# Keeping x in SBUF through layer 0 and passing gate rows through DRAM in a two-block fp32 transformer kernel

## The chip, the cores and the metric

One core of one Trainium2 chip runs the whole program. The metric is the device time of one launch in microseconds (us); less is better. The trace names the engines PE (TensorE, matmuls), PEld (its weight loads), DVE (VectorE), ACT (ScalarE), POOL (GpSimd) and SP (SyncE). A DMA is issued by an instruction in one of the queues; the rows ACTq and SPq are such issues.

## The reference

All is fp32, with 256 latent tokens (x), 256 context tokens (cx) and a model width D of 1024. A first block of two layers attends over both; a second block of two layers has ffn, mix, ffn. Cut to what matters here:

```python
def layer(x, cx, ...):                        # first block, twice
    mod = c_silu @ ada_w + ada_b              # shift, scale, gate: 1024 each
    shift, scale, gate = jnp.split(mod, 3, axis=-1)
    hx = rmsnorm(x, norm_w) * (1 + scale[:, None, :]) + shift[:, None, :]
    ...                                       # three kinds of attention -> ux, uc
    x = x + gate[:, None, :] * (ux @ w_out)
    if need_ctx:                              # layer 0 alone
        cx = cx + gate_c * (uc @ w_out)

def second_block(x, ...):                     # twice
    x = x + 0.5 * swiglu(rms(x, ffn1_norm), wg, wu, wd)
    h = rms(x, mix_norm)
    (q_a, g_a, kc, vc, ...) = split_cols(h @ w_in)
    y_a = nsa(...)    # compresses kc and vc: gelu(flat @ w1) @ w2
    y_b = moba(...)
    x = x + (sigmoid(gate_a) * y_a + sigmoid(gate_b) * y_b) @ w_out
    x = x + 0.5 * swiglu(rms(x, ffn2_norm), ...)
return rms(x, final_norm)
```

## The kernel before

The weights of all products come as one stream of tiles, mostly 128x1024 words (512 KB), in the order of a plan. `_dma` (L260) puts the fetch of a tile `ws` into SP's queue, at most four tiles ahead of the splits. `_split` splits a tile into a rounded part `wh`, cast by ACT (L286), and a rest `wl = ws - wh`, by DVE (L287), two tiles ahead of their use; there are three buffers of each, so a cast waits until PE is done with the tile three before it. For each weight block `three` issues three matmuls: wh with the high part of the activations (L426), wl with the high part (L427), wh with the low part (L428). PE works through the stages in order: the two layers of the first block (in the trace to about 752 us), then ffn1, mix and ffn2 of both layers of the second block. A scheduler at build time orders the instructions of each engine from their dependencies and from which pool's memory is free. So a row of an engine's stream need not stand where its line is called.

Three places bear on the change:

- **The end of a layer of the first block** (`w_out`). Matmuls over the gated attention output fill four accumulators; `add` multiplies each by the gate row (DVE, `tmp`, L1123) and adds it to x or cx (L1124). The gate is held as a column per 128 values, `mod`. To get it as a row on every partition, L1116 multiplies each column, spread over 128 columns, with the identity, and DVE copies the result to the tile `gt` (L1117). In layer 0 the gated products of the attention (names `sg`) live in the memory of x, of cx and of one more tile; `uc` (L1107 on ACT, L1108 on DVE) are the parts of them for the context tokens, and x and cx are loaded again from DRAM (L1110) before `add`.
- **The start of mix.** Its first product `h @ w_in` needs x transposed: PE turns 128x128 blocks of x with the identity (L467), ACT and DVE split them into `xt` (L474, L475). The weights of the compression, two tiles `w1` of 128x2048 words and a small `w2`, are fetched from ACT's queue in the text's order at the start of mix (L1205, L1218); the `w1` tiles share tags (`big0`, `big1`) with later tiles of mix.
- **The pools.** `sink` and `nsink` are two tiles of 8 words a partition; the row `fw2` of the final norm is fetched at the second stage of the second block (L1518).

Of the kernel before, what the change touches and what calls it, by code (L numbers as in the profile page):

```python
# [19 lines left out]
P = 128  # L20
# [4 lines left out]
HD = 64  # L25
# [203 lines left out]
class Body:  # L229
# [526 lines left out]
    def ada_close(self, g):  # L756

        nc = self.nc
        nb = len(g["blocks"])
        self.uid += 1  # L760
        m = self.junk.tile([P, 512], F32, tag="junk", name=f"mod{self.uid}")
        nc.scalar.copy(m[:4 * nb, :], g["bank"][:4 * nb, :])
        p = self.ps("r")
        for j in range(4):
            nc.tensor.matmul(p[:, 16 * j:16 * j + 2 * nb], m[:4 * nb, j * P:(j + 1) * P],
                             self.cst("sel2")[:4 * nb, :2 * nb], start=True, stop=True)
        pv = p[:, :64].rearrange("p (j b s) -> p s b j", b=8, s=2)
        b = 0
        while b < nb:
            l, c0 = g["blocks"][b]  # L770
            e = b + 1
            while e < nb and g["blocks"][e] == (l, c0 + 512 * (e - b)):
                e += 1
            for s in range(2):
                o = c0 // P
                nc.vector.tensor_tensor(self.mod[l][:, s, o:o + 4 * (e - b)].rearrange("p (b j) -> p b j", j=4),
                                        pv[:, s, b:e, :],
                                        self.col("ada_b", 24 * l + o, 4 * (e - b)).rearrange("p (b j) -> p b j", j=4), op=ALU.add)
                a, z = max(o, 8), min(o + 4 * (e - b), 16)
                if a < z:  # L780
                    nc.vector.scalar_tensor_tensor(self.mod[l][:, s, a:z], self.mod[l][:, s, a:z], 1.0,
                                                   self.col("norm_w", 8 * l + a - 8, z - a), op0=ALU.add, op1=ALU.mult)
            b = e

    def norm_rows(self, x, dst):
# [34 lines left out]
    def block1(self, x):  # L820
        nc, tc = self.nc, self.tc
        cx = self.cx1
        with ExitStack() as es:
            hp = es.enter_context(tc.tile_pool(reuse_waits="tile", name="hT", bufs=1))
            hT = self.new_hT(hp, 0)
            with tc.tile_pool(reuse_waits="tile", name="w0", bufs=START_TILES) as self.w0:
                self.start(x, cx, hT)
            for l in range(DEPTH):
                if l:
                    self.psum("L1")  # L830
                hT = self.layer1(l, x, cx, hT, hp)

    def start(self, x, cx, hT):

# [7 lines left out]
        nc.vector.tensor_copy(self.ident_r, self.ident)  # L842
        self.norm_rows(x, x)
        self.norm_rows(cx, cx)

        def half(h):
            for c in (4 * h, 4 * h + 2):
                for s, v in enumerate((x, cx)):
                    self.mod_pair(0, s, c, self.turn_pair(v, c), hT)
# [31 lines left out]
    def layer1(self, l, x, cx, hT, hp):  # L881
# [3 lines left out]
        with ExitStack() as lay:  # L885
            lp = lay.enter_context(tc.tile_pool(reuse_waits="tile", name=f"lay{l}", bufs=1))
            if need:
                sg2 = lp.tile([P, 4, T], F32, name="sg2")
                xv, cv = (t.rearrange("p t (a d) -> p (t a) d", d=T) for t in (x, self.cx1))

                def sg(c, n):
                    return (xv, cv, sg2)[c // 4][:, c % 4:c % 4 + n, :]
            else:
                sg2 = lp.tile([P, 4, T], F32, name="sg2b")
                cv1 = self.cx1.rearrange("p t (a d) -> p (t a) d", d=T)

                def sg(c, n, sg2=sg2, cv1=cv1):
                    return cv1[:, c:c + n, :] if c < 8 else sg2[:, c - 8:c - 8 + n, :]
# [10 lines left out]
            qn = lp.tile([P, 2, HD], F32, name=f"qn{l}")  # L909
            sink = lp.tile([P, 8], F32, name=f"sink{l}")  # L910
            nc.scalar.dma_start(qn[:, 0, :], self.row_bcast(self.dram["k_norm_a"], l * HD, HD))
            nc.scalar.dma_start(qn[:, 1, :], self.row_bcast(self.dram["q_norm_a"], l * HD, HD))
            nc.scalar.dma_start(sink, self.row_bcast(self.dram["sink_c"], l * 8, 8))
            nsink = lp.tile([P, 8], F32, name=f"nsink{l}")
            nc.vector.tensor_scalar(nsink, sink, -1.0, None, op0=ALU.mult)
# [184 lines left out]
            with tc.tile_pool(reuse_waits="tile", name=f"wo{l}", bufs=1) as wp:  # L1100
                gate = wp.tile([P, 2, D], F32, name=f"gt{l}")
                tmp = wp.tile([P, 4, 512], F32, name=f"tmp{l}")
                if need:
                    uc = [wp.tile([P, 12, 256], F32R, name=f"uc{j}") for j in range(2)]
                    for c in [c for ks in WOUT_KS for c in ks]:
                        g = sg(c, 1)[:, 0, 256:512]
                        nc.scalar.copy(uc[0][:, c, :], g)  # L1107
                        nc.vector.tensor_tensor(uc[1][:, c, :], g, uc[0][:, c, :].bitcast(F32), op=ALU.subtract)  # L1108
                    for t, nm in ((x, "x"), (cx, "ctx")):
                        nc.sync.dma_start(t, self.dram[nm].rearrange("o (t p) d -> p (o t) d", p=P))  # L1110
                for s in range(2 if need else 1):
                    for ct in range(2):
                        p = self.ps("x")
                        for j in range(4):
                            g = self.mod[l][:, s, 16 + 4 * ct + j:17 + 4 * ct + j]
                            nc.tensor.matmul(p[:, j * P:(j + 1) * P], g.to_broadcast([P, P]), self.ident, start=True, stop=True)  # L1116
                        nc.vector.tensor_copy(gate[:, s, ct * 512:ct * 512 + 512], p)  # L1117

# [25 lines left out]


    def ffn(self, l, name, x, xt, ss, hooks, after):

        nc, tc = self.nc, self.tc
        with tc.tile_pool(reuse_waits="tile", name=f"f{name}{l}", bufs=1) as fp, tc.tile_pool(reuse_waits="tile", name=f"g{name}{l}", bufs=2) as gp, \
# [5 lines left out]
            for fi, (c0, n) in enumerate(FFN_COLS):  # L1155
                a = self.gemm(name + "_wg_2", l, c0, xt[0], xt[1], toks, KD, hooks if fi == 0 else None)
                if r is None:
                    r = ss() if callable(ss) else self.finish_rstd(ss, 2)
                s = gp.tile([P, 2, 512], F32, tag="s", name=f"s{name}{l}{fi}")
                for t in range(2):  # L1160
# [27 lines left out]
    def mix(self, l, x, xt, ss, hooks, after):  # L1188
        nc, tc = self.nc, self.tc
        with ExitStack() as es:  # L1190
# [11 lines left out]
            toks = [(0, None), (1, None)]  # L1202
            w1 = [op.tile([P, 16, P], F32, tag=f"big{j}", name=f"w1{l}_{j}") for j in range(2)]
            for j, nm in enumerate(("cmpk_w1_2", "cmpv_w1_2")):
                nc.scalar.dma_start(w1[j], self.dram[nm][l].rearrange("(m p) j -> p m j", p=P))  # L1205
            oT = {k: [op.tile([P, 4, 256], F32R, name=f"o{k}{l}_{j}") for j in range(2)] for k in "NM"}
# [8 lines left out]
            Vb = mp.tile([64, 2, 4, 64], F32, name=f"Vb{l}")  # L1215
            w2 = mp.tile([P, 2, HD], F32, name=f"w2{l}")
            o2 = COLS["w2"][0] + P * l
            nc.scalar.dma_start(w2, self.dram["cols"][:, o2:o2 + P].rearrange("p (a d) -> p a d", a=2))  # L1218
            graw = []
# [201 lines left out]
            for mi, (kind, b) in enumerate(MIX):  # L1421
# [7 lines left out]
                if kind in ("ga", "gb"):  # L1429
                    while len(graw) < 2:  # L1430
                        graw.append(op.tile([P, 2, D], F32, tag=f"big{len(graw)}", name=f"graw{l}_{len(graw)}"))
                    for t in range(2):
# [60 lines left out]
    def block2(self, x, out):  # L1493
# [18 lines left out]
        for i, (l, s) in enumerate(stages):  # L1512
            ss = first_scale if i == 0 else ops[i][1]
            args = (x, ops[i][0], ss, {4: lambda i=i: self.b2_half(i, 1)} if i else None, lambda h, i=i: self.b2_half(i + 1, h))
            self.psum(s)
            if i == 1:
                fw = bp.tile([P, D], F32, tag="xtrow", name="fw2")
# [17 lines left out]
    def run(self, out):  # L1535
        nc, tc = self.nc, self.tc
        with ExitStack() as es:
# [14 lines left out]
            self.ident = self.cst("ident")  # L1552
            self.ident_r = cp.tile([P, P], F32R, name="ident_r")
            self.mod = [cp.tile([P, 2, 24], F32, name=f"mod{l}") for l in range(DEPTH)]

# [74 lines left out]
```

## Time and profile before

| | before |
|---|---|
| time, median of 3 runs | 1947.4 us (1946.05 to 1948.95) |
| the profiled execution's own time | 1947.63 us |
| its span in the trace | 1945.8 us |
| PE busy | 1904.4 us, 98% of the span |
| DVE, ACT busy | 1279.4 us (66%), 1103.3 us (57%) |
| DMA | 294.62 MB, mean 151 GB/s |

The span runs from the first to the last recorded instruction; 1.8 us of the execution's time lie around it. PE's busy time is that of modelled ends, so 98% says that PE is nearly always fed, and not that it runs at its peak.

### The profile page before, as it was taken

To read this page: it belongs to the slowest core of one execution; us is meant where nothing else is said; L and a number is where in the kernel's file an instruction comes from. 1 tells how busy PE (TensorE), PEld (TensorE's weight loads), DVE (VectorE), ACT (ScalarE), POOL (GpSimd) and SP (SyncE) were. 2 spreads that over 40 slices of the span, in tenths; PEclk is the share of its full clock that TensorE was granted. 3 is DMA by queue.
4 is the path that set the end of the run, shared out by engine and by line. 5 is a ranking of instruction groups with operands and counts; after the bars stand their busy time and mean duration, and the time that the engine had idled before them with its cause. 6 is when DMAs were issued, how large, how long until landed. Compare 5 with 4: busy or idle time off the path is not lost.

```text
span 1945.8 us, 27694 instructions
## 1 busy us (share of the span) xinstructions
PE 1904.4 (98%) x10348; PEld 1561.0 (80%) x10348; DVE 1279.4 (66%) x2490; ACT 1103.3 (57%) x1979; POOL 1.0 (0%) x7
## 2 busy tenths in 40 slices
PE   8999999999999999999899999999999899999998
PEld 3777778777988877888788878888888788888886
DVE  5486856788596787555689575555555588675555
ACT  4367657775567675444467645445444458655443
POOL 0000000000000000000000000000000000000000
PEclk9999999999999999999999999999999999999999
DMA  7333324135422236554523565554555433456552
GB/s 304 106 123 130 118 90 150 55 131 186 136 93 95 85 109 216 184 184 141 166 93 125 164 215 198 183 191 173 193 186 173 144 106 101 152 180 234 186 181 74
DMA packets 85270, 294.62 MB, mean 151 GB/s; under 512 B 10000, under 2 KB 10384, under 8 KB 85136
## 3 DMA queue, kind: packets, MB, share of 16 engines
q1 hardware_dynamic: 80432, 283.39, 43.0%
q10 hardware_dynamic: 4704, 9.47, 1.5%
q8 instruction: 81, 1.33, 0.3%
q14 instruction: 53, 0.43, 0.1%
HBM read 291.77 MB, written 1.05 MB: 150 GB/s over the span
## 4 chain that ended last, share of the span: by engine, by line
PE 92%; DVE 4%; ACT 2%; issue 1%; ACTq 1%; DMA 1%; SPq 0%; DVEq 0%
PE acc L426 24%; PE acc L428 24%; PE acc L427 24%; PE pso L609 4%; PE pst L580 4%; PE pss L514 2%; PE pss L515 2%; PE psr L715 1%; DVE wl L287 1%; PE psx L1173 1%; ACT wh L286 1%; PE psr L721 1%; PE psm L747 1%; PE psm L1260 1%; PE acc L750 1%
## 5 line engine op out<-in xcount | busy, mean ns | idle before, releaser
L287 DVE TENSOR_TENSOR wl<-ws,wh 128x1024 fp32r<-128x1024 f32 (+2 forms) x538 | 638.1, 1188 | 478.8 <-ACT wh L286 476.0
L286 ACT CAST wh<-ws 128x1024 fp32r<-128x1024 f32 (+2 forms) x538 | 549.2, 1024 | 573.3 <-PE acc L428 503.3
L426 PE MATMUL acc<-wh,xt 128*128 128x512 f32 (+3 forms) x1120 | 419.6, 376 | 11.7 <-ACT wh L286 11.7
L427 PE MATMUL acc<-wl,xt 128*128 128x512 f32 (+3 forms) x1120 | 416.6, 372 | 0.0
L428 PE MATMUL acc<-wh,xt 128*128 128x512 f32 (+3 forms) x1120 | 416.4, 373 | 0.0
L426 PEld LDWEIGHTS acc<-wh,xt 128*128 128x128 f32 x1120 | 212.1, 190 | 44.9 <-ACT wh L286 12.9
L428 PEld LDWEIGHTS acc<-wh,xt 128*128 128x128 f32 x1120 | 211.8, 189 | 33.0 <-issue 0.7
L427 PEld LDWEIGHTS acc<-wl,xt 128*128 128x128 f32 x1120 | 212.7, 190 | 31.2 <-issue 0.3
L426 PE MATMUL acc<-wh,hT 128*128 128x384 f32 (+2 forms) x480 | 159.6, 333 | 0.1
L427 PE MATMUL acc<-wl,hT 128*128 128x384 f32 (+2 forms) x480 | 158.5, 330 | 0.0
L428 PE MATMUL acc<-wh,hT 128*128 128x384 f32 (+2 forms) x480 | 158.1, 329 | 0.0
L550 ACT ACTIVATE p<-pss,nm 128x512 f32<-128x512 f32 (+2 forms) x240 | 127.5, 539 | 20.3 <-DVE nm L546 5.1
L426 PE MATMUL acc<-wh,hffn 128*128 128x512 f32 x352 | 137.7, 391 | 0.0
L428 PE MATMUL acc<-wh,hffn 128*128 128x512 f32 x352 | 137.1, 389 | 0.0
L427 PE MATMUL acc<-wl,hffn 128*128 128x512 f32 x352 | 137.0, 389 | 0.0
L580 PE MATMUL pst<-consts,p 128*128 128x128 f32 x624 | 103.3, 278 | 0.0
L427 PEld LDWEIGHTS acc<-wl,hT 128*128 128x128 f32 x480 | 90.6, 189 | 7.2 <-issue 1.9
L426 PEld LDWEIGHTS acc<-wh,hT 128*128 128x128 f32 x480 | 90.5, 189 | 6.8 <-issue 0.8
L428 PEld LDWEIGHTS acc<-wh,hT 128*128 128x128 f32 x480 | 90.5, 189 | 5.8 <-issue 1.2
L580 PEld LDWEIGHTS pst<-consts,p 128*128 128x128 f32 x624 | 72.2, 140 | 28.5 <-ACT p L572 5.6
L572 ACT ACTIVATE p<-p,rinv 128x256 f32<-128x256 f32 (+2 forms) x152 | 81.5, 573 | 16.5 <-DVE rinv L566 12.2
L428 PEld LDWEIGHTS acc<-wh,hffn 128*128 128x128 f32 x352 | 66.1, 188 | 13.9
(318 smaller groups left out, 2868.5 us busy)
## 6 DMA issues: line engine op xcount, KB each, us to landing
ws<-in_wall SPq DMA_DIRECT2D x476, 512.0 KB, 3.4
ws<-in_wall SPq DMA_DIRECT2D x64, 384.0 KB, 3.1
bias<-in_bias ACTq DMA_DIRECT2D x8, 512.0 KB, 4.0
x<-in_x SPq DMA_DIRECT2D x2, 1024.0 KB, 6.5
cx<-in_ctx SPq DMA_DIRECT2D x2, 1024.0 KB, 10.3
ws<-in_wall SPq DMA_DIRECT2D x4, 420.0 KB, 3.0
out<-y SPq DMA_DIRECT2D x2, 512.0 KB, 2.6
ws<-in_wall SPq DMA_DIRECT2D x2, 280.0 KB, 2.8
```

The source lines that it names most:

```text
L286: self.nc.scalar.copy(h[:, :n], s[:, :n])
L287: self.nc.vector.tensor_tensor(lo[:, :n], s[:, :n], h[:, :n].bitcast(F32), op=ALU.subtract)
L426: mm(out, ah, bh, start=start, stop=False)
L427: mm(out, ah, bl, start=False, stop=False)
L428: mm(out, al, bh, start=False, stop=stop)
L514: nc.tensor.matmul(S[:, o:o + w], q, kh, start=True, stop=False)
L515: nc.tensor.matmul(S[:, o:o + w], q, kl, start=False, stop=True)
L550: nc.scalar.activation(p[:, o:o + w], S[:, o:o + w], AF.Exp, bias=nm[:, i:i + 1], accum_out=sm[:, i:i + 1])
L572: nc.scalar.activation(p[:, o:o + w], p[:, o:o + w], AF.Copy, scale=r[:, i:i + 1])
L580: nc.tensor.transpose(t[:, i * P:(i + 1) * P], sl["P"][:, o:o + P], self.ident)
L609: nc.tensor.matmul(O[HD * i:HD * i + HD, c:c + m * P], v, u["pt"][:, b:b + m, :].rearrange("p m t -> p (m t)"), start=k == 0, stop=k == nk ...
L715: nc.tensor.transpose(p[:, 2 * a + g, :], ks[:, t, a, g, :], self.ident_r)
```

## The change

- x is no longer used as memory for gated products. A tile `sg0` of its own takes its place in layer 0; the normalised rows of the start go to two new tiles (`xn0`) that are freed after the start. The reload of x at the end of layer 0 goes; that of cx stays.
- The gate columns are written to a DRAM tile from POOL's queue as soon as they exist (`gate_rows`), and read back as a row on all partitions from ACT's queue (L1124 of the changed kernel). The 48 products L1116 and the 6 copies L1117 go.
- The compression weights are fetched by `cmp_load`, called in the second part of ffn1, into tiles of the pool of the whole second block.
- `sink` and `nsink` are parts of one tile of 64 words; `fw2` is fetched one stage later in the text.

```diff
+            if c0 >= 2 * D:
+                self.gate_rows(l, c0 - 2 * D, 512 * (e - b))
             b = e
+
+    def gate_rows(self, l, c0, n):
+
+        if l not in self.gates:
+            self.gates[l] = self.gp.tile([2, KD, P], F32, name=f"gates{l}")
+        c = c0 // P
+        for s in range(2 if l == 0 else 1):
+            self.nc.gpsimd.dma_start(self.gates[l][s, c:c + n // P, :].rearrange("j p -> p j"), self.mod[l][:, s, 16 + c:16 + c + n // P])
...
-        self.norm_rows(x, x)
-        self.norm_rows(cx, cx)
+        xn, cn = (xp.tile([P, 2, D], F32, name=f"xn0_{j}") for j in range(2))
+        self.norm_rows(x, xn)
+        self.norm_rows(cx, cn)
...
-                sg2 = lp.tile([P, 4, T], F32, name="sg2")
-                xv, cv = (t.rearrange("p t (a d) -> p (t a) d", d=T) for t in (x, self.cx1))
+                sgs = [lp.tile([P, 4, T], F32, name="sg0"), cx.rearrange("p t (a d) -> p (t a) d", d=T),
+                       lp.tile([P, 4, T], F32, name="sg2")]
...
-            sink = lp.tile([P, 8], F32, name=f"sink{l}")
+            sinks = lp.tile([P, 64], F32, name=f"sink{l}")
+            sink, nsink = sinks[:, :8], sinks[:, 8:16]
...
-                    for t, nm in ((x, "x"), (cx, "ctx")):
-                        nc.sync.dma_start(t, self.dram[nm].rearrange("o (t p) d -> p (o t) d", p=P))
+                    nc.sync.dma_start(cx, self.dram["ctx"].rearrange("o (t p) d -> p (o t) d", p=P))
                 for s in range(2 if need else 1):
-                    for ct in range(2):
-                        p = self.ps("x")
-                        for j in range(4):
-                            g = self.mod[l][:, s, 16 + 4 * ct + j:17 + 4 * ct + j]
-                            nc.tensor.matmul(p[:, j * P:(j + 1) * P], g.to_broadcast([P, P]), self.ident, start=True, stop=True)
-                        nc.vector.tensor_copy(gate[:, s, ct * 512:ct * 512 + 512], p)
+                    g = self.gates[l][s:s + 1].rearrange("s j p -> s (j p)")
+                    nc.scalar.dma_start(gate[:, s, :], g.to_broadcast([P, D]))
...
+    def cmp_load(self, l):
+
+        nc = self.nc
+        w1 = [self.bp.tile([P, 16, P], F32, tag=f"big{j}", name=f"w1{l}_{j}") for j in range(2)]
+        for j, nm in enumerate(("cmpk_w1_2", "cmpv_w1_2")):
+            nc.scalar.dma_start(w1[j], self.dram[nm][l].rearrange("(m p) j -> p m j", p=P))
+        w2 = self.bp.tile([P, 2, HD], F32, tag="w2", name=f"w2{l}")
+        o2 = COLS["w2"][0] + P * l
+        nc.scalar.dma_start(w2, self.dram["cols"][:, o2:o2 + P].rearrange("p (a d) -> p a d", a=2))
+        self.cmp_w = w1, w2
...
+                if fi == 1 and name == "ffn1":
+                    self.cmp_load(l)
...
-            w1 = [op.tile([P, 16, P], F32, tag=f"big{j}", name=f"w1{l}_{j}") for j in range(2)]
-            for j, nm in enumerate(("cmpk_w1_2", "cmpv_w1_2")):
-                nc.scalar.dma_start(w1[j], self.dram[nm][l].rearrange("(m p) j -> p m j", p=P))
+            w1, w2 = self.cmp_w
...
-            if i == 1:
+            if i == 2:
                 fw = bp.tile([P, D], F32, tag="xtrow", name="fw2")
```

**Where the compression weights are issued.** In the kernel before, ACT's queue at the start of the first mix (about 940 us) reads as follows; `w10_0` and `w10_1` are the two w1 tiles of layer 0, `w20` its w2.

```order
L286 CAST wh230_9936<-ws230_9868 128x840
L286 CAST wh231_9954<-ws231_9886 128x840
L1205 DMA w10_0_10014<-in_cmpk_w1_2 128x16x128
L1205 DMA w10_1_10015<-in_cmpv_w1_2 128x16x128
L1218 DMA w20_10034<-in_cols 128x128
L286 CAST wh232_10038<-ws232_9904 128x560
L286 CAST wh233_10064<-ws233_9922 128x768
```

The three issues stand between two casts of the weight stream, and the second mix has the same rows. In the changed kernel they are gone from there, and layer 0's stand in ACT's queue at the end of layer 1 of the first block, some 70 tiles earlier (`gt1` is that layer's gate row, `w10_0` and the rest as above).

```order
L286 CAST wh160_8292<-ws160_8053 128x1024
L596 COPY pt_1356_8248<-pst1354_8240 128x4x128
L1158 DMA w10_0_8803<-in_cmpk_w1_2 128x16x128
L286 CAST wh161_8310<-ws161_8126 128x1024
L977 CAST u1_0_7923<-cx1_84 128x256
L1124 DMA gt1_8345<-gates1_2507 128x1024
L286 CAST wh162_8348<-ws162_8212 128x1024
L1158 DMA w10_1_8804<-in_cmpv_w1_2 128x16x128
L286 CAST wh163_8366<-ws163_8278 128x1024
L286 CAST wh164_8413<-ws164_8296 128x1024
L1161 DMA w20_8807<-in_cols 128x128
L482 ACTIVATE junk1361_8409,xss0_8388<-x_79 128x512
```

Nothing holds these back but earlier work on ACT. Layer 1's `w11` tiles stand in the last product of the first mix, each between two casts, and wait there for the last reader of the tile whose memory they take.

**The end of layer 0.** DVE's order before, from the last of 12 `uc` rows to the first split of the context product (`wl100`); `acc670` and `acc671` are the accumulators of the first half of x:

```order
L1108 TENSOR_TENSOR uc1_4743<-cx1_84,uc0_4742 128x256
L1117 COPY gt0_4740<-psx798_4776 128x512
L1117 COPY gt0_4740<-psx799_4782 128x512
L287 TENSOR_TENSOR wl99_4813<-ws99_4477,wh99_4812 128x1024
L1117 COPY gt0_4740<-psx800_4788 128x512
L1123 TENSOR_TENSOR tmp0_4741<-acc670_4141,gt0_4740 128x512
L1123 TENSOR_TENSOR tmp0_4741<-acc671_4142,gt0_4740 128x512
L1124 TENSOR_TENSOR x_79<-x_79,tmp0_4741 128x512 x2
L287 TENSOR_TENSOR wl100_4835<-ws100_4540,wh100_4834 128x1024
```

And in the changed kernel, at the same place:

```order
L1120 TENSOR_TENSOR uc1_4756<-cx1_84,uc0_4755 128x256
L1130 TENSOR_TENSOR tmp0_4754<-acc670_4154,gt0_4753 128x512
L1130 TENSOR_TENSOR tmp0_4754<-acc671_4155,gt0_4753 128x512
L1131 TENSOR_TENSOR x_79<-x_79,tmp0_4754 128x512 x2
L287 TENSOR_TENSOR wl100_4825<-ws100_4553,wh100_4824 128x1024
```

The copies are gone and `wl99` has moved ahead of the `uc` rows; `tmp`, which now waits for the gate DMA, still stands ahead of `wl100`. That DMA waits for PE's last attention product (L609), whose memory its tile takes. On PE, between that product and the first matmul with `wl100`, 41 matmuls and 16 of the L1116 stood before, and 26 matmuls stand now; the other 15 are ahead of it.

## Rows read from the trace of the kernel before

**Rows 1.** Page, chain that ended last: share of the span by engine

```profile
PE 92%; DVE 4%; ACT 2%; issue 1%; ACTq 1%; DMA 1%; SPq 0%; DVEq 0%
```

**Rows 2.** Timeline of PE: start, length, instruction, [idle time before <- releaser]

```profile
949.56 0.97 PE L426 MATMUL acc<-wh,xt 128*128 128x384 f32 x2 [4.97 <-ACT wh L286]
...
1542.27 0.97 PE L426 MATMUL acc<-wh,xt 128*128 128x384 f32 x2 [5.14 <-ACT wh L286]
...
753.78 0.41 PE L467 MATMUL psx<-consts,x 128*128 128x128 f32 x2 [1.69 <-DVE x L1124]
...
1163.50 0.96 PE L426 MATMUL acc<-wh,xt 128*128 128x512 f32 x3 [0.53 <-ACT wh L286]
...
49.95 1.05 PE L765 MATMUL psr<-consts,mod 8*128 8x4 f32 x8 [1.41 <-ACT mod L762]
```

**Rows 3.** Timeline of ACT and its queue, start of the first mix

```profile
941.48 3.07 ACTq L1205 DMA_DIRECT2D w<-in_cmpv_w  x1
944.59 3.41 ACTq L1218 DMA_DIRECT2D w<-in_cols  x1
948.12 1.39 ACT L286 CAST wh<-ws 128x560 fp32r<-128x560 f32 x2 [6.67 <-issue]
```

**Rows 4.** Windows: length, busy PE, PEld, DVE, ACT, POOL; PEclk, DMA share, GB/s

```profile
944.50:949.50 5.00, 0.09 (x1) 0.00 (x0) 0.69 (x1) 1.38 (x3) 0.00 (x0) 0.71 1.05 291
949.50:955.00 5.50, 5.44 (x26) 4.97 (x27) 4.65 (x18) 3.52 (x10) 0.00 (x0) 0.65 0.66 206
...
1542.20:1547.40 5.20, 5.13 (x19) 4.68 (x20) 4.27 (x17) 3.50 (x10) 0.00 (x0) 0.51 0.60 191
...
756.00:758.00 2.00, 2.00 (x10) 1.63 (x10) 1.82 (x9) 1.91 (x3) 0.00 (x0) 1.00 0.94 311
...
54.00:56.00 2.00, 1.86 (x7) 1.27 (x6) 1.97 (x6) 1.29 (x3) 0.00 (x0) 0.50 0.57 231
```

**Rows 5.** Chain, end of layer 0: start, length, engine, tile, line

```profile
441.69 0.43 DVE cx L988
...
442.72 1.48 DVE uc L1108 x5
...
444.31 2.43 DVE uc L1108 x7
...
447.94 1.13 DVE wl L287
...
449.59 1.28 DVE tmp L1123 x2
...
453.26 0.50 PE acc L427
453.76 0.23 PE acc L428
```

**Rows 6.** Chain, end of layer 1: the L1116 products there

```profile
737.70 1.79 PE psx L1116 x16
```

**Rows 7.** Line L1110 (reload of x and cx): from issue to landing

```profile
DMA to landing us min/median/max: 4.9/6.5/8.2
```

**Rows 8.** Tile fw (rows of 4 KB spread over all partitions): from issue to landing

```profile
DMA to landing us min/median/max: 4.2/5.7/7.1
```

**Rows 9.** Timeline of ACT, end of layer 1

```profile
736.14 0.41 ACT L965 CAST u<-cx 128x256 fp32r<-128x256 f32 x1 [2.77 <-DVE cx L988]
...
742.33 1.05 ACT L286 CAST wh<-ws 128x1024 fp32r<-128x1024 f32 x1 [3.55 <-PE acc L428]
...
748.75 1.05 ACT L286 CAST wh<-ws 128x1024 fp32r<-128x1024 f32 x1 [0.21 <-ACT xt L474]
```

**Rows 10.** Timeline of DVE: layer 0's gate columns, and the gating of layer 1

```profile
327.25 0.24 DVE L776 TENSOR_TENSOR mod<-psr,cols 128x8 f32<-128x8 f32 x2 [0.91 <-PE psr L765]
...
744.56 1.28 DVE L1123 TENSOR_TENSOR tmp<-acc,gt 128x512 f32<-128x512 f32 x2
```

**Rows 11.** Page, DMA queues: packets, MB, share of 16 engines over the span

```profile
q10 hardware_dynamic: 4704, 9.47, 1.5%
```

More of the change, by code (lines that the diff above doesn't have):

```diff
@@ L825, in block1 @@
             hT = self.new_hT(hp, 0)
-            with tc.tile_pool(reuse_waits="tile", name="w0", bufs=START_TILES) as self.w0:
-                self.start(x, cx, hT)
+            with tc.tile_pool(reuse_waits="tile", name="w0", bufs=START_TILES) as self.w0, \
+                    tc.tile_pool(reuse_waits="tile", name="xn0", bufs=1) as xp:
+                self.start(x, cx, hT, xp)
             for l in range(DEPTH):
@@ L831, in block1, with start @@
                 hT = self.layer1(l, x, cx, hT, hp)
-    def start(self, x, cx, hT):
+    def start(self, x, cx, hT, xp):
         nc, tc = self.nc, self.tc
@@ L842, in start @@
         nc.vector.tensor_copy(self.ident_r, self.ident)
-        self.norm_rows(x, x)
-        self.norm_rows(cx, cx)
+        xn, cn = (xp.tile([P, 2, D], F32, name=f"xn0_{j}") for j in range(2))
+        self.norm_rows(x, xn)
+        self.norm_rows(cx, cn)
         def half(h):
             for c in (4 * h, 4 * h + 2):
-                for s, v in enumerate((x, cx)):
+                for s, v in enumerate((xn, cn)):
                     self.mod_pair(0, s, c, self.turn_pair(v, c), hT)
@@ L887, in layer1 @@
             if need:
-                sg2 = lp.tile([P, 4, T], F32, name="sg2")
-                xv, cv = (t.rearrange("p t (a d) -> p (t a) d", d=T) for t in (x, self.cx1))
+                sgs = [lp.tile([P, 4, T], F32, name="sg0"), cx.rearrange("p t (a d) -> p (t a) d", d=T),
+                       lp.tile([P, 4, T], F32, name="sg2")]
                 def sg(c, n):
-                    return (xv, cv, sg2)[c // 4][:, c % 4:c % 4 + n, :]
+                    return sgs[c // 4][:, c % 4:c % 4 + n, :]
             else:
@@ L913, in layer1 @@
             nc.scalar.dma_start(sink, self.row_bcast(self.dram["sink_c"], l * 8, 8))
-            nsink = lp.tile([P, 8], F32, name=f"nsink{l}")
             nc.vector.tensor_scalar(nsink, sink, -1.0, None, op0=ALU.mult)
@@ L1215, in mix @@
             Vb = mp.tile([64, 2, 4, 64], F32, name=f"Vb{l}")
-            w2 = mp.tile([P, 2, HD], F32, name=f"w2{l}")
-            o2 = COLS["w2"][0] + P * l
-            nc.scalar.dma_start(w2, self.dram["cols"][:, o2:o2 + P].rearrange("p (a d) -> p a d", a=2))
             graw = []
@@ L1430, in mix @@
                     while len(graw) < 2:
-                        graw.append(op.tile([P, 2, D], F32, tag=f"big{len(graw)}", name=f"graw{l}_{len(graw)}"))
+                        graw.append(self.bp.tile([P, 2, D], F32, tag=f"big{len(graw)}", name=f"graw{l}_{len(graw)}"))
                     for t in range(2):
@@ L1553, in run @@
             self.ident_r = cp.tile([P, P], F32R, name="ident_r")
+            self.gates = {}
+            self.gp = pool("gates", 1, space=bass.MemoryType.DRAM)
             self.mod = [cp.tile([P, 2, 24], F32, name=f"mod{l}") for l in range(DEPTH)]
```

## The prediction, on record before the changed kernel ran

> **What bounds the kernel now.** I read the chain of work first: 92% of the span is PE, ACT's queue and "issue" hold 1% each [rows 1]. So PE's own work is the floor, and an edit pays only by taking work off PE or by ending a wait of PE. I then read PE's timeline for the longest waits after the start of the program. Two stand out, at the start of each mix: 4.97 us at 949.56 and 5.14 us at 1542.27, both until a cast of `wh` [rows 2]. ACT's timeline tells why that cast is late: ACT itself sat in the issues of the compression weights, 3.07 us in that of the second `w1` and 3.41 us in that of `w2`, and the cast at 948.12 follows them with 6.67 us of idle time put down to "issue" [rows 3]. The windows show what comes after: PE is busy again for 5.44 of 5.50 us, but at a granted clock of 0.65, and for 5.13 of 5.20 us at 0.51 after the second wait [rows 4]. Between the two levels of 1.2 and 2.4 GHz these are mixtures: the clock fell while PE stood still (0.71 already in the idle window) and came back after some us of work. So each wait costs twice, once as idle time and once as slow matmuls.
>
> **The compression weights.** The order of the changed kernel has no issue left between the casts at the start of either mix. What remains of the wait is what the other stage entries show: 0.53 us at 1163.50, for a `wh` cast at the same place of ffn2; the same 0.53 stands at two more entries [rows 2]. I expect that:
>
> - idle time: 4.97 - 0.53 = 4.44 and 5.14 - 0.53 = 4.61, together 9.05 us;
> - clock: (1 - 0.65) x 5.44 = 1.90 and (1 - 0.51) x 5.13 = 2.51, together 4.41 us, since a wait of 1.69 us (at 753.78) left the window behind it at 1.00 [rows 2, 4].
>
> The sum is 13.5 us. At best nothing is left of the waits: 10.11 + 4.41 = 14.5. At worst each mix keeps a wait of 1.69, the longest of any other stage entry: 10.11 - 3.38 + 4.41 = 11.1.
>
> Where do the issues go? Layer 1's two `w1` stand between casts in the last product of the first mix. An issue can hold ACT 3.07 to 3.41 us there [rows 3]. Splits run two tiles ahead, and a tile is 12 matmuls of 0.23 us there, so 5.5 us of PE's work hide one issue. Priced at nothing; without that cover it is what it was, some 5 us of idle time and 2 of clock. Layer 0's stand in the end of layer 1, priced below.
>
> A rule of the Trainium skill speaks against all this. "DMA: Bandwidth & Descriptors", section "Issuing engines are not separate DMA queues", says that the sequencer time it takes to initiate a DMA is usually small relative to the DMA itself. By it, three issues could not hold ACT for 6.67 us, and moving them would give nothing: the sum would be 1.4 us and not 14.9. The trace doesn't agree here: the issue instructions themselves last 3.07 and 3.41 us [rows 3]. I go by the row.
>
> **The end of layer 0.** 32 of the products L1116 go, at 1.79 us per 16 [rows 6]: 3.6 us of PE work. But PE is not what ends last here. The order puts 15 matmuls of 0.23 us ahead of the last attention product and takes 16 L1116 from there, so that product, which ended where DVE's `cx` row starts at 441.69, ends at 441.69 + 3.45 - 1.79 = 443.35. From there DVE has `cx` 0.43, twelve `uc` in 1.48 + 2.43, two `tmp` 1.28, two additions to x at the same price, and `wl100` 1.13 [rows 5]: 451.4. PE has 26 matmuls, so it is done at 449.4 and waits. It restarted at 453.26 before [rows 5]: a gain of 1.9 if the gate row is there at 447.7, when the first `tmp` wants it. The DMA is issued at 443.4 at the earliest. Its price is bounded by 4.2 us (a spread row) [rows 8] and by 4.9 and 8.2 (x and cx, 1 MB each, at this very place) [rows 7]. With 4.2 it is hidden, with 8.2 `tmp` starts at 451.6 and PE at 455.3, a loss of 2.0. Two gate rows and cx are together the bytes that x and cx were; I take 5.5, near x's, which puts PE at 452.6: **a gain of 0.7**. PE then stands still for 3.2 us, between the 1.69 that left the clock alone and the 4.97 that didn't. At the start of the program waits of 1.41 us and less were followed by a window at 0.50 [rows 2, 4]. I charge nothing and keep a loss of 1.9 to 2.5 for the range.
>
> **The end of layer 1.** 16 products go, 1.79 us of PE's work on the chain [rows 6]. ACT now issues `w10_0`, the gate row after the cast of `u` at 736.14, `w10_1` ahead of the cast at 742.33, and `w20` two casts on [rows 9]. The gate row lands 4.2 to 8.2 us after 736.6, at 740.8 to 744.8; `tmp` wants it at 744.56 - 1.79 = 742.8 [rows 10]: up to 2.0 lost. `w10_1` is covered by the splits ahead. `w20`, if it holds ACT 3.41 us as before, pushes the cast at 748.75; ahead of that cast ACT had 0.2 to 0.6 us of slack, and behind it hang `wl`, `tmp`, the addition and the PE wait at 753.78. That is a loss of up to 2.8. I take **a gain of 0.7**, with +1.8 and -1.0 as bounds.
>
> **The rest.** The gate columns are written by POOL, which has no other work, over 100 us before they are read. The normalised rows at the start get other tiles and the same instructions in the same order. `sink` in one tile is the same instruction. `fw2` and two other small loads move by a few rows to places well ahead of their readers. If one of these covers were gone, its cost would be a landing of 4 to 8 us on PE.
>
> **Sum.** 13.5 + 0.7 + 0.7 = 14.9 us off the profiled execution's 1947.63 (span 1945.8 and 1.8 around it) is 1932.7. That execution is 0.2 above the median of 1947.4, so **1932.6** for the median.
>
> **The rivals.**
>
> - *The wait moves to the end of layer 1.* ACT sits in the `w20` issue, the wait at 753.78 grows from 1.69 to 4.5 us and the clock falls behind it: 13.5 + 0.7 - 1.0 - 2.5 = 10.7 gained, 1936.8. For it: the issues of rows 3 lasted 3 us with another large one just ahead, and two stand ahead here. Against: casts stand between them now, so that the first has time to drain.
> - *The mixes keep half.* Each keeps 1.69 us, now for `xt`, and half the clock loss: 10.11 - 3.38 + 2.2 + 1.4 = 10.3, 1937.2. For it: the transposes of x end just before the wait and `xt` follows. Against: 0.53 at the other entries.
> - *No change.* The ACT time isn't the issue's own but a wait for whatever else the DMA engines do (share 1.05 in that window [rows 4]), and it returns where the issues went: 1.4 or less gained, 1946. The rule above leads to the same number.
> - *Slower: the gate columns land late.* They are written in pieces of 4 bytes, 2048 for layer 0. Queue q10 had 4704 packets in 1.5% of 16 engines' 1945.8 us [rows 11], 99 ns each on its engine. Spread over 16 engines 2048 take 13 us; one after the other on a single engine 203 us. From 327.5, where the columns exist [rows 10], to 443, where the read is issued, are 115 us. So one engine would make PE wait 88 us: 2021. It decides from 115 + 15 = 130 us on, 63 ns a piece in series. I know of no row that shows such a write; that two engines are enough to hide it speaks against it. The Trainium skill, same page, "Rules for kernel authors", has a strided last dimension lowered to one descriptor per element, and advises against it; no run here shows it yet.
>
> **Chances and range.** The forecast 0.62, the wait at the end of layer 1 0.14, half kept 0.12, no change 0.07, slower 0.05. The forecast's own bounds run from 14.5 + 1.9 + 1.8 = 18.2 gained (1929.3) to 11.1 - 2.0 - 1.0 = 8.1 (1939.4); both of the smaller gains lie inside. So 1929.5 to 1939.5. A difference of 0.2% (3.9 us) is about what a measurement of this kernel can tell from none. Faster by more: 0.62 + 0.14 + 0.12 = 0.88; within it 0.07; slower 0.05.
>
> **What the profile after would show.** At the start of both mixes no ACT issue, a PE wait near 0.5 us and a clock of 1.00 in the 5 us behind it. At the end of layer 0 a PE wait of about 3 us until `wl100`, and whether the clock falls. At the end of layer 1 how long the `w10` and `w20` issues last and whether the wait before L467 grew past 1.69. In POOL's rows three writes that land well before 443. The prediction is wrong if ACT's issues last 3 us in their new places and PE waits there, or if the mix still waits over 2 us.

## The result and the profile after

The changed kernel takes 1930.81 us (median, 1929.5 to 1932.53) against 1946.8 us for the kernel before in the same rounds (1946.05 to 1948.95): a ratio of 0.9917, interval 0.9899 to 0.9934, 16.0 us faster. The forecast was 1932.6, with a range of 1929.5 to 1939.5. The profiled execution's span fell from 1945.8 to 1930.7, by 15.1 us.

The page of the changed kernel, busy time and then three lines of its DMA queues (packets, MB, share of 16 engines):

```profile
PE 1896.2 (98%) x10300; PEld 1551.9 (80%) x10300; DVE 1275.7 (66%) x2484; ACT 1103.2 (57%) x1979; POOL 3.8 (0%) x10
...
q10 hardware_dynamic: 5136, 11.04, 1.8%
...
q0 software_dynamic: 96, 0.01, 0.1%
```

PE has 8.2 us less busy time; the rest of the gain is time in which it no longer waits. q0 is new: the three writes of gate columns.

The timeline of PE of the changed kernel, for its longest waits after the start:

```profile
453.90 0.50 PE L427 MATMUL acc<-wl,uc 128*128 128x512 f32 x1 [1.83 <-DVE wl L287]
...
752.29 0.41 PE L467 MATMUL psx<-consts,x 128*128 128x128 f32 x2 [1.10 <-DVE x L1131]
...
943.57 0.44 PE L427 MATMUL acc<-wl,xt 128*128 128x384 f32 x1 [0.34 <-DVE wl L287]
...
1155.01 0.97 PE L426 MATMUL acc<-wh,xt 128*128 128x512 f32 x3 [0.52 <-ACT wh L286]
...
1530.02 0.44 PE L427 MATMUL acc<-wl,xt 128*128 128x384 f32 x1 [0.34 <-DVE wl L287]
```

The waits of 4.97 and 5.14 us at the starts of mix [rows 2] are down to 0.34 each, and for another releaser. The wait at the end of layer 0 is new, that at the end of layer 1 is shorter (1.69 before). The windows of the changed kernel, behind the wait at the end of layer 0 and behind the two starts of mix (columns as in [rows 4]):

```profile
451.50:454.00 2.50, 0.63 (x3) 0.29 (x2) 2.50 (x5) 2.13 (x5) 0.00 (x0) 1.00 0.88 351
454.00:458.00 4.00, 4.00 (x18) 3.31 (x19) 4.00 (x6) 1.50 (x3) 0.00 (x0) 1.00 0.70 194
...
944.00:950.00 6.00, 6.00 (x40) 5.92 (x40) 3.91 (x8) 4.91 (x9) 0.00 (x0) 1.00 0.50 169
...
1530.00:1536.00 6.00, 5.98 (x38) 5.69 (x39) 4.27 (x8) 4.52 (x7) 0.00 (x0) 1.00 0.47 127
```

The granted clock is 1.00 (2.4 GHz) in all of them, where it was 0.65 and 0.51 behind the waits of before. Where the issues went, ACT and its queue at the end of layer 1:

```profile
730.46 0.85 ACTq L1158 DMA_DIRECT2D w<-in_cmpk_w  x1
...
735.82 0.34 ACTq L1124 DMA_DIRECT2D gt<-gates  x1
737.33 1.05 ACT L286 CAST wh<-ws 128x1024 fp32r<-128x1024 f32 x1 [1.19 <-PE acc L428]
...
737.39 0.73 ACTq L1158 DMA_DIRECT2D w<-in_cmpv_w  x1
...
742.78 1.06 ACT L286 CAST wh<-ws 128x1024 fp32r<-128x1024 f32 x1 [1.61 <-PE acc L428]
742.79 0.34 ACTq L1161 DMA_DIRECT2D w<-in_cols  x1
```

The same three issues that took 0.85, 3.07 and 3.41 us at 940 [rows 3] take 0.85, 0.73 and 0.34 here, with casts between them that wait for PE and not for them.

The end of layer 0 on DVE in the changed kernel:

```profile
445.65 0.42 DVE L1000 TENSOR_TENSOR cx<-pso,cx 128x256 f32<-128x256 f32 x1 [1.28 <-PE pso L609]
...
449.68 0.42 DVE L1120 TENSOR_TENSOR uc<-cx,uc 128x256 fp32r<-128x256 f32 x1
450.22 1.29 DVE L1130 TENSOR_TENSOR tmp<-acc,gt 128x512 f32<-128x512 f32 x2
451.43 1.28 DVE L1131 TENSOR_TENSOR x<-x,tmp 128x512 f32<-128x512 f32 x2
452.63 2.35 DVE L287 TENSOR_TENSOR wl<-ws,wh 128x1024 fp32r<-128x1024 f32 x2
```

The chain cx, uc, tmp, x, `wl100` is what PE waits for, and `tmp` follows the last `uc` row with a gap of 0.1 us: the gate row is there when it is wanted, but only just. Its read is issued at 446.17 and lands 4.0 us later, at 450.13, and `tmp` starts at 450.22. Lines L793 (the writes) and L1124 (the reads) of the changed kernel:

```profile
L793 POOL DMA_DIRECT2D gates<-mod x3: 883/886/1020, 252.2 to 330.3; - x3
...
DMA to landing us min/median/max: 10.3/10.3/10.3
```

```profile
L1124 ACTq DMA_DIRECT2D gt<-gates x3: 338/340/444, 446.2 to 735.8; - x3
...
DMA to landing us min/median/max: 4.0/4.5/4.8
```

### The profile page after: what moved, and what is told of

The parts are those of the page before. It is cut to its first block, busy times and chain, and to the rows that moved or that the text cites. A ratio compares the mean times of both kernels' runs of the same rounds, so it can differ in the third digit from the quotient of the medians.

```text
span 1930.7 us, 27566 instructions
## 1 busy us (share of the span) xinstructions
PE 1896.2 (98%) x10300; PEld 1551.9 (80%) x10300; DVE 1275.7 (66%) x2484; ACT 1103.2 (57%) x1979; POOL 3.8 (0%) x10
## 4 chain that ended last, share of the span: by engine, by line
PE 71%; DVE 3%; ACT 1%; issue 1%; DMA 0%; ACTq 0%; DVEq 0%
PE acc L428 20%; PE acc L426 20%; PE acc L427 20%; PE pst L580 2%; PE pso L609 2%; PE pss L514 1%; PE pss L515 1%; PE psx L1193 1%; DVE wl L287 1%; PE psr L715 1%; PE psm L1275 1%; ACT wh L286 1%; PE psx L467 0%; PE psr L721 0%; PE psm L1362 0%
## 5 line engine op out<-in xcount | busy, mean ns | idle before, releaser
L426 PE MATMUL acc<-wh,xt 128*128 128x512 f32 (+3 forms) x1120 | 417.6, 374 | 1.7 <-ACT wh L286 1.6
L428 PE MATMUL acc<-wh,xt 128*128 128x512 f32 (+3 forms) x1120 | 414.8, 372 | 0.0
L426 PEld LDWEIGHTS acc<-wh,xt 128*128 128x128 f32 x1120 | 210.5, 188 | 34.7 <-ACT wh L286 2.3
L428 PEld LDWEIGHTS acc<-wh,xt 128*128 128x128 f32 x1120 | 210.6, 188 | 33.2 <-issue 0.7
L426 PE MATMUL acc<-wh,hT 128*128 128x384 f32 (+2 forms) x480 | 159.5, 333 | 0.0
L428 PE MATMUL acc<-wh,hT 128*128 128x384 f32 (+2 forms) x480 | 158.1, 329 | 0.0
L426 PE MATMUL acc<-wh,hffn 128*128 128x512 f32 x352 | 137.8, 391 | 0.0
L428 PE MATMUL acc<-wh,hffn 128*128 128x512 f32 x352 | 137.1, 390 | 0.0
L426 PEld LDWEIGHTS acc<-wh,hT 128*128 128x128 f32 x480 | 90.5, 189 | 6.6 <-issue 0.8
L428 PEld LDWEIGHTS acc<-wh,hT 128*128 128x128 f32 x480 | 90.5, 189 | 5.6 <-issue 1.2
L428 PEld LDWEIGHTS acc<-wh,hffn 128*128 128x128 f32 x352 | 66.1, 188 | 14.0
```

What stands on the lines that cost most here:

```text
L426: mm(out, ah, bh, start=start, stop=False)
L428: mm(out, al, bh, start=False, stop=stop)
```

## Marks: the gain by stages

Five PE rows stand in every kernel's trace: the L428 matmul near 100 us with a wait of some 1.25 us for `wl` (start), the L715 row near 540 with 0.43 us (end of layer 0), the first L426 of 280 columns near 940 (start of mix), and the L467 rows with 0.33 us near 1150 and 1740 (end of the first and second mix). The table has the differences of their start times, in us, and from the first mark to the end of the span.

| kernel | layer 0 | layer 1, ffn1 | first mix | ffn2, ffn1, second mix | mark to end |
|---|---|---|---|---|---|
| before | 443.20 | 396.51 | 215.78 | 593.27 | 1844.9 |
| changed | 441.17 | 394.50 | 209.67 | 586.48 | 1828.1 |
| undo_cmp | 441.27 | 394.55 | 215.80 | 593.15 | 1841.1 |
| only_cmp | 442.39 | 396.41 | 209.80 | 586.47 | 1831.3 |
| undo_gates | 443.99 | 396.40 | 209.68 | 586.42 | 1832.5 |
| w2_first | 442.86 | 396.44 | 210.94 | 588.04 | 1834.4 |
| only_gates | 445.95 | 394.50 | 215.59 | 593.31 | 1845.7 |
| only_x | 443.59 | 396.33 | 216.06 | 593.13 | 1845.1 |
| cmp_pool | 442.62 | 396.39 | 210.57 | 587.92 | 1833.9 |
| w1_contig | 443.47 | 396.41 | 210.30 | 587.04 | 1833.4 |
| undo_x | 445.52 | 394.41 | 209.69 | 586.46 | 1832.4 |
| after_again | 440.68 | 394.37 | 209.66 | 586.45 | 1827.5 |
| uc_gt | 440.20 | 395.23 | 209.66 | 586.43 | 1827.9 |

In layer 0 kernels that are alike there (before, only_cmp, w2_first, cmp_pool, w1_contig) spread over 1.1 us; their mean is 442.9, that of the three with both edits of layer 0 (changed, undo_cmp, after_again) 441.0, so the gain of that column is better put at 1.9. In the other columns the spread of like kernels is 0.2, and 0.5 in the first mix where the issues stand there. From before to changed: layer 0 gains 2.0, layer 1 2.0, the mixes 6.1 and 6.8, together 16.9 from the mark on (16.8 to the end). The first mark itself stands 1.67 us later (102.57 against 100.90), which makes 15.1.

That start doesn't look like the change's doing: over 13 executions the mark stands between 98.20 and 102.57, with the early and the late ones among kernels with and without the new tiles (only_gates 98.25, only_x 98.47, w2_first 102.07). The first 360 rows or more of ACT, DVE and PE are the same work in the same order in before and changed. What differs is the clock behind the short waits of the start; a window of the changed kernel and then of undo_gates:

```profile
54.00:62.00 8.00, 7.47 (x23) 5.54 (x23) 5.13 (x15) 2.74 (x6) 0.00 (x0) 0.57 0.29 114
```

```profile
54.00:62.00 8.00, 7.95 (x37) 6.42 (x36) 3.95 (x11) 3.92 (x7) 0.00 (x0) 0.99 0.08 34
```

## The experiments

**undo_cmp**: the compression weights back at the start of mix.

```diff
-                if fi == 1 and name == "ffn1":
-                    self.cmp_load(l)
...
-            w1, w2 = self.cmp_w
+            w1 = [op.tile([P, 16, P], F32, tag=f"big{j}", name=f"w1{l}_{j}") for j in range(2)]
+            for j, nm in enumerate(("cmpk_w1_2", "cmpv_w1_2")):
+                nc.scalar.dma_start(w1[j], self.dram[nm][l].rearrange("(m p) j -> p m j", p=P))
```

> The changed kernel with the compression weights fetched again from ACT's queue at the start of mix; x resident and the gate rows through DRAM stay. Theory (ACT sits in its DMA issues and holds the wh cast): both mix waits of about 5 us and the slow clock behind them return, 13.8 us of the 15.1 gained between the traces are lost, so about 1944.5 us and slightly under the kernel before. Rival (the gain comes from the gate rows and from x staying resident): under 4 us are lost, about 1934.

Measured: 1943.8 us, 0.999 of before (0.998 to 0.9999). The waits are back with 4.55 and 4.54 us, the clock behind the first is at 0.51 (a window, columns as in [rows 4]), and both mix stages have the times of before.

```profile
945.66 0.97 PE L426 MATMUL acc<-wh,xt 128*128 128x384 f32 x2 [4.55 <-ACT wh L286]
...
1538.19 0.97 PE L426 MATMUL acc<-wh,xt 128*128 128x384 f32 x2 [4.54 <-ACT wh L286]
```

```profile
945.60:950.60 5.00, 4.94 (x19) 4.49 (x20) 4.26 (x17) 3.30 (x10) 0.00 (x0) 0.51 0.84 246
```

The rival falls: without this part the change is worth 2 us by the times, 3.8 by the marks.

**only_cmp**: the compression weights alone moved, in the kernel before (the diff's `cmp_load` parts).

> The kernel before with the compression weights alone moved, as in the change. Theory: 13 to 14 us faster than before, 1933 us, mix waits near 0.4 us. Rival (the end of layer 1 can't take the issues without the time that the dropped gate products free there): a wait of over 2 us appears ahead of the transposes at about 754 us and the gain is 10 us or less.

Measured: 1933.15 us, 0.9935 (0.9921 to 0.9948), 12.2 us faster; 13.6 by the marks, 12.8 of it in the two mix stages. The column of layer 1 says that the new place costs 0.1 us at most (396.41 and 396.51, and with the gate rows 394.50 and 394.55): the rival falls too, though `w2` was held 2.67 us there. It was issued 1.5 us after the second `w1`; in the changed kernel 5.4 us lie between the two, and `w2` takes 0.34.

**undo_gates**: the changed kernel with the products L1116 and the copies L1117 back.

```diff
-                    g = self.gates[l][s:s + 1].rearrange("s j p -> s (j p)")
-                    nc.scalar.dma_start(gate[:, s, :], g.to_broadcast([P, D]))
+                    for ct in range(2):
+                        p = self.ps("x")
+                        for j in range(4):
+                            g = self.mod[l][:, s, 16 + 4 * ct + j:17 + 4 * ct + j]
+                            nc.tensor.matmul(p[:, j * P:(j + 1) * P], g.to_broadcast([P, P]), self.ident, start=True, stop=True)
+                        nc.vector.tensor_copy(gate[:, s, ct * 512:ct * 512 + 512], p)
```

> The changed kernel with the gate products on PE and their copies on DVE back, no gate rows in DRAM. Theory: the gate rows brought about 3 us (2.0 at the end of layer 0 and 1.1 at the end of layer 1 by the two traces), so about 1934 us. Rival (PE's 5.4 us for 48 products were all on the path): 5 us or more slower, 1936. Second rival (those products filled waits of PE, and x resident alone gave the gain at the end of layer 0): within 1 us, 1931 to 1932.

Measured: 1933.02 us, 0.9937 (0.9924 to 0.9949), 2.2 us over the changed kernel by medians, which were not taken in the same rounds, 3.9 by the two ratios (0.9917 and 0.9937, whose intervals overlap); by the marks 4.3 us slower, with 2.8 more in layer 0 and 1.9 more in layer 1. The theory's 3 us lie inside these, the first rival's 5 just above them. The second rival (x resident gave the gain of layer 0) falls: layer 0 takes 443.99 with x resident and the gate products back, no less than before.

**w2_first**: the kernel before with the small `w2` issued ahead of the two `w1`.

```diff
+            w2 = mp.tile([P, 2, HD], F32, name=f"w2{l}")
+            o2 = COLS["w2"][0] + P * l
+            nc.scalar.dma_start(w2, self.dram["cols"][:, o2:o2 + P].rearrange("p (a d) -> p a d", a=2))
             w1 = [op.tile([P, 16, P], F32, tag=f"big{j}", name=f"w1{l}_{j}") for j in range(2)]
...
-            w2 = mp.tile([P, 2, HD], F32, name=f"w2{l}")
-            o2 = COLS["w2"][0] + P * l
-            nc.scalar.dma_start(w2, self.dram["cols"][:, o2:o2 + P].rearrange("p (a d) -> p a d", a=2))
```

> The kernel before with the small w2 issued ahead of the two w1 at the start of each mix; nothing else moves. Theory (an ACT issue is held only while a large one stands just ahead of it): w2 takes about 0.35 us, the first w1 0.85, the second w1 again 3.1 to 3.4; ACT comes to the cast 3 us earlier, PE waits 1.5 to 2.5 us instead of 5, 6 us or more gained in all, up to 10 if the clock holds, so 1937 to 1941 us. Rival (what holds ACT is the landing of the same 2.1 MB, in whatever order): same waits, same time as before.

Measured: 1937.43 us, 0.9955 (0.994 to 0.997), 7.9 us faster (10.5 by the marks), with the PE waits at 0.49 and 0.79 us: the rival falls. ACT's queue at the start of the first mix:

```profile
941.10 0.33 ACTq L1205 DMA_DIRECT2D w<-in_cols  x1
941.66 0.85 ACTq L1208 DMA_DIRECT2D w<-in_cmpk_w  x1
942.97 1.32 ACTq L1208 DMA_DIRECT2D w<-in_cmpv_w  x1
944.38 1.39 ACT L286 CAST wh<-ws 128x560 fp32r<-128x560 f32 x2 [1.45 <-issue]
```

The small load takes 0.33 us with nothing ahead of it and 3.41 with two large ones ahead. The second `w1` is held too, but 1.32 (1.74 in the second mix) and not 3.1 to 3.4: that part of the expectation was wrong.

**cmp_pool**: the kernel before with the same three loads at the same place, issued from POOL's queue (`nc.gpsimd.dma_start` for `nc.scalar.dma_start`).

> The kernel before with the compression weights issued at the same place, at the start of mix, but from POOL's queue. The same 2.1 MB move at the same time; ACT issues nothing. Theory (ACT held in its own issues): mix waits under 1 us, clock 1.00 behind them, 11 to 13 us faster, 1933 us. Rival (the transfer itself holds the weight stream; the DMA share was 1.05 there): waits of over 3 us stay, 1943 to 1945.

Measured: 1933.66 us, 0.9932 (0.9918 to 0.9945). PE's waits there:

```profile
942.87 0.44 PE L427 MATMUL acc<-wl,xt 128*128 128x384 f32 x1 [0.66 <-DVE wl L287]
...
1530.05 0.44 PE L427 MATMUL acc<-wl,xt 128*128 128x384 f32 x1 [0.52 <-DVE wl L287]
```

The same bytes move within a microsecond of when they did before: in the 5 us from 941.10 the DMA share is 1.03, as it was 1.05 in the wait of before [rows 4], while the clock stays at 1.00. At the old place PE hardly waits; one more wait, 1.28 us for DVE's `Z`, stands 12 us behind in the second mix. So the transfer was not the cause, the issue on ACT was.

**w1_contig**: the kernel before with each `w1` read as 128 runs of 8 KB.

```diff
-                nc.scalar.dma_start(w1[j], self.dram[nm][l].rearrange("(m p) j -> p m j", p=P))
+                nc.scalar.dma_start(w1[j], self.dram[nm][l].rearrange("(p m) j -> p m j", p=P))
```

> The kernel before with the two w1 read as 128 runs of 8 KB each in place of 2048 runs of 512 bytes, same bytes, same place, same queue. The compression then multiplies by rows in another order, so that part of the computation is changed. Theory (the number of pieces holds the issue): each issue takes 0.3 to 0.5 us, mix waits under 1 us, 11 to 13 us faster, 1933 us. Rival (the bytes in flight hold it): the third issue still lasts 2 us or more and waits of over 3 us stay.

Measured: 1933.12 us, 0.9932 (0.9919 to 0.9946). Its issues by lines L1205 and L1218 (ns min/median/max):

```profile
L1205 ACTq DMA_DIRECT2D w<-in_cmpk_w x2: 334/334/334, 940.0 to 1527.1; - x2
...
L1205 ACTq DMA_DIRECT2D w<-in_cmpv_w x2: 450/450/451, 940.4 to 1527.4; - x2
```

```profile
L1218 ACTq DMA_DIRECT2D w<-in_cols x2: 335/394/453, 940.9 to 1528.2; - x2
```

Same bytes, same queue, same order, and no issue is held. What held ACT was that the loads ahead came in many small pieces, 2048 of 512 bytes each, and not their megabyte. Number and size of the pieces changed together here, so which of the two counts is not shown.

**only_gates**: the gate rows alone, in the kernel before, x still reloaded.

> The kernel before with the gate rows alone changed: written to DRAM from POOL, read back on ACT's queue, no gate products. Theory (by the marks in the traces so far, 2.0 us at the end of layer 1 and 1 to 2.8 at the end of layer 0): 3 to 4.5 us faster, about 1941.5. Rival (with x reloaded at the same moment the gate row lands later than 4.5 us and holds DVE): under 1.5 us faster, 1944 to 1945.

Measured: 1945.73 us, 0.9998 (0.9989 to 1.0007): no difference. Layer 1 gains the 2.0 us, layer 0 loses 2.7. DVE at the end of layer 0, then the PE wait that follows, then the windows behind it:

```profile
445.10 1.29 DVE L1129 TENSOR_TENSOR tmp<-acc,gt 128x512 f32<-128x512 f32 x2 [0.46 <-DMA gt<-gates]
448.87 1.29 DVE L1130 TENSOR_TENSOR x<-x,tmp 128x512 f32<-128x512 f32 x2 [2.48 <-DMA x<-in_x]
450.08 2.35 DVE L287 TENSOR_TENSOR wl<-ws,wh 128x1024 fp32r<-128x1024 f32 x2
```

```profile
451.35 0.80 PE L427 MATMUL acc<-wl,uc 128*128 128x512 f32 x1 [4.39 <-DVE wl L287]
```

```profile
451.40:455.00 3.60, 3.60 (x9) 2.83 (x10) 3.60 (x6) 0.00 (x0) 0.00 (x0) 0.50 0.47 112
455.00:460.00 5.00, 5.00 (x20) 3.99 (x19) 2.62 (x7) 3.03 (x6) 0.00 (x0) 0.82 0.69 247
```

The gate row is 0.46 us late. What is late next is x: DVE waits 2.48 us for its reload with `wl100` queued behind, PE waits 4.39, and the clock falls to 0.50. Both my theory and the rival (a late gate row) missed this.

**only_x**: x resident alone, in the kernel before.

> The kernel before with x alone kept in SBUF (its own tile for gated products, two tiles for the normalised rows, the sinks in one tile, the final-norm row one stage later). Theory: the reload of x was hidden, so nothing is gained; the marks say 0 to 1 us slower, 1945.4 to 1946.4. Rival (the reload landed when DVE wanted x): 2 us or more faster.

Measured: 1945.17 us, 0.9994 (0.9985 to 1.0003), and 0.2 us by the marks. In the kernel before the reload was hidden, so ending it pays nothing by itself. Layer 0 is not untouched, though: the last `cx` row comes 1.3 us later behind the first mark (342.12 against a mean of 340.8 in the kernels that are alike there), and the stretch behind the restart is shorter, as told below.

**undo_x**: the changed kernel with x's memory used for gated products and x reloaded.

> The changed kernel with x not kept in SBUF: x's memory holds gated products again and x is reloaded at the end of layer 0; the gate rows through DRAM and the moved compression weights stay. Theory (the gate rows pay at the end of layer 0 only if x needn't be reloaded): a PE wait of 4 us or more there until the reload of x has landed, the clock at 0.5 behind it, 3.5 to 5 us slower than the changed kernel, 1933 to 1935 us. Rival (that wait in the kernel with the gate rows alone came from a chance of that one execution): under 1.5 us slower.

Measured: 1934.03 us, 0.9938 (0.9925 to 0.9952), against **after_again**, the changed kernel in the same rounds:

> The changed kernel again, in the same rounds as the two others of this call, as the mark they are held against: 0.991 to 0.993 of the kernel before.

It had 1930.81 us, 0.9922 (0.9909 to 0.9934). By medians undo_x is 3.2 us slower (the intervals of the two touch), by the marks 4.9, 4.8 of it in layer 0. DVE and PE of undo_x:

```profile
452.17 1.29 DVE L1130 TENSOR_TENSOR x<-x,tmp 128x512 f32<-128x512 f32 x2 [2.54 <-DMA x<-in_x]
```

```profile
454.65 0.79 PE L427 MATMUL acc<-wl,uc 128*128 128x512 f32 x1 [4.32 <-DVE wl L287]
```

The wait for x is there again: it was no chance of one execution.

**uc_gt**: the changed kernel with the gate tile in memory of its own and four of the twelve `uc` subtractions on POOL.

```diff
-                gate = wp.tile([P, 2, D], F32, name=f"gt{l}")
+                gate = lp.tile([P, 2, D], F32, name=f"gt{l}")
...
-                        nc.vector.tensor_tensor(uc[1][:, c, :], g, uc[0][:, c, :].bitcast(F32), op=ALU.subtract)
+                        e = nc.gpsimd if c // 4 == 1 else nc.vector
+                        e.tensor_tensor(uc[1][:, c, :], g, uc[0][:, c, :].bitcast(F32), op=ALU.subtract)
```

> The changed kernel with the gate row's tile in memory of its own, so that its DMA is issued long before the end of layer 0, and four of the twelve uc subtractions on POOL. Theory (DVE's chain of uc, tmp, x and wl100 is all that holds PE there): the PE wait of 1.83 us falls under 0.6, 1 to 1.8 us faster than the changed kernel, 1929 to 1930. Rival (POOL's subtractions are slow, or slow DVE's beside them): the wait stays at 1.5 us or more, same time as the changed kernel or slower.

Measured: 1928.93 us, 0.9919 (0.9905 to 0.9932), which the intervals can't tell from after_again. PE's waits in it:

```profile
449.56 0.50 PE L427 MATMUL acc<-wl,uc 128*128 128x512 f32 x1 [0.63 <-DVE wl L287]
...
747.82 0.41 PE L467 MATMUL psx<-consts,x 128*128 128x128 f32 x2 [2.04 <-DVE x L1132]
```

The wait at the end of layer 0 fell nearly as expected, from 1.83 to 0.63, and layer 0 is 0.5 us shorter, less than its column scatters. At the end of layer 1 the wait grew from 1.10 to 2.04 and the column is 0.9 us longer; the earlier gate row probably let the scheduler reorder that place too, which no run of its own shows. The two cancel. Which of the two edits shortened the first wait is open as well.

## Why the prediction was right, step by step

**The mixes.** The mechanism was the one that the forecast named, and undo_cmp, only_cmp and cmp_pool show it: ACT sits in its own DMA issues, with a `wh` cast behind them that PE needs. Forecast 13.5, measured 6.1 + 6.8 = 12.9. Idle time was worth 4.63 + 4.80 = 9.4 (forecast 9.05), so the clock gave 3.5 and not 4.41. That 3.5 is what the two columns leave over, not a time read by itself. That the clock costs extra is seen in the waits that were kept: behind 4.55 us in undo_cmp it was at 0.51, behind 1.83 in the changed kernel at 1.00.

**The rule of the Trainium skill** ("DMA: Bandwidth & Descriptors", "Issuing engines are not separate DMA queues": initiating a DMA is usually small beside it). The trace agrees for loads of few pieces: issues of 0.33 to 0.45 us in w1_contig, beside 5.1 to 8.2 from issue to landing. It does not for a load issued right behind loads of 2048 pieces: 3.07 and 3.41 [rows 3], beside landings of 7.1 to 10.4. Here the exception was worth 13 us.

**The end of layer 0**, forecast 0.7, measured 1.9 (2.0 in the first trace, 2.5 in after_again). The term was sized wrong, and its total hides three misses. First, the step "I take 5.5, near x's" for the landing of the gate row: the first row of layer 0 took 4.0 us (3.8 in after_again and undo_cmp), and `tmp` was hardly held. That it fitted is in part luck, for landing and the end of the `uc` rows fall within 0.1 us of each other; the second row took 4.8. So DVE's chain sets PE's restart, PE waits 1.83 us and not 3.2, and the clock holds. Second, a hidden landing was forecast to gain 1.9 at the restart, and 1.2 came (means of the like kernels, from the first mark), since the last `cx` row stood 0.6 us later than forecast.

Third, the other 0.7 lies behind the restart, where the forecast had nothing. The same matmuls with `uc` stand there in both kernels, and the distance between them differs; a stretch of 45 steps, before and then changed:

```profile
454.07 0.40 PE L428 MATMUL acc<-wh,uc 128*128 128x512 f32 x1
...
464.57 0.39 PE L428 MATMUL acc<-wh,uc 128*128 128x512 f32 x1
```

```profile
454.70 0.40 PE L428 MATMUL acc<-wh,uc 128*128 128x512 f32 x1
...
464.92 0.39 PE L428 MATMUL acc<-wh,uc 128*128 128x512 f32 x1
```

That is 0.233 us a matmul before and 0.227 after, at a granted clock of 1.00 in both, and there are 144 of them. All seven kernels that reload x have the longer distance behind the restart, and all six that keep it the shorter one. The edits around x also give other tiles another place in memory; whether that is the cause no run tests.

The forecast had no term for x resident. In front of its own DVE chain it priced the addition to x at its duration only; the runs show that the chain could run this early only because x was already there. Each of the two edits alone is worth nothing in the times (0.9994, 0.9998); together, in undo_cmp, layer 0 is 1.9 us shorter than before, and undo_x puts the price of bringing the reload back at 4.8: 2.2 up to the restart, 2.1 at the slow clock behind it, and 0.5 in the longer distance of the matmuls.

**The end of layer 1**, forecast 0.7, measured 2.0. The bound "`w20`, if it holds ACT 3.41 us as before" did not come true: 0.34 us, with casts that wait for PE between the issues. The gate row landed within 5.5 us in the traces of the changed kernel, ahead of `tmp`. What was left is the whole of the 16 products, 1.79 by [rows 6], and 0.2 more.

**The start** was forecast at nothing, which holds as to the change; in the profiled execution it took 1.67 us, a scatter that kernels with and without the change show.

So 13.5 + 0.7 + 0.7 = 14.9 became 12.9 + 2.0 + 2.0 = 16.9, less 1.7 of scatter in the trace. That the profiled span fell by 15.1, so near the 14.9, is luck: misses of -0.6, +1.3, +1.3 and -1.7 cancel. The median fell by 16.0. The forecast's last step has a slip of 0.1: 14.9 off a median of 1947.4 is 1932.5. The rivals: the wait did not move to the end of layer 1; the mixes kept 0.34 and not 1.69; "no change" falls with only_cmp. The slower rival, gate columns landing late, was off by far: the writes landed 10.3 us after their issue, near the 13 us forecast for pieces spread over the engines, with 115 us at hand. The Trainium skill advises against a strided last dimension (same page, "Rules for kernel authors"), since it is lowered to one descriptor per element. The profile has 32 packets for each write of 1024 words and doesn't tell descriptors; the writes held up nothing here.

## What to carry to other kernels

An engine that issues a DMA can be held in the issue while the loads just ahead of it are in many small pieces; if that engine also feeds the bottleneck, use fewer and longer pieces, put the small load first, spread the issues between waits, or issue from an idle engine: each of the four took away most of the 5 us waits here. Price a wait of the matmul engine at more than its length when it is as long as 4 us: in every such case here the clock was low behind it. And when work is taken off a chain, ask which transfer that the work used to cover is wanted next: the gate rows paid in layer 0 only because x no longer had to be reloaded.

## What the runs showed of the hardware that was not expected

- Two issues of loads with 2048 pieces of 512 bytes, back to back on ACT's queue, held the second for 2.51 to 3.40 us and a small third load for 3.36 to 3.46 (before, undo_cmp and only_gates); with the small load first the second large one was held for 1.32 and 1.74 (w2_first). The same bytes in 128 pieces each took 0.33 to 0.45. POOL took 1.15 to 1.30 us for the large ones, and none of PE's waits there ends on POOL.
- Three writes of 1024 words each, from 128 partitions to DRAM, went out as 96 packets together (q0), and each landed 10.3 us after its issue.
- The same matmuls of 512 columns, with `uc` as their moving input, followed each other every 0.233 us in the seven kernels that reload x and every 0.227 in the six that keep it, at a clock of 1.00; the cause is open.
- Behind waits of 4.3 to 5.1 us the clock stood at 0.50 to 0.65 in all cases looked at, and behind waits of 1.7 and 1.8 us in none; but at the start of the program, with several waits of 1.4 us and less in a row, it fell in some executions (0.57) and not in others (0.99), for a scatter of some 4 us at the first mark.
